# A hybrid attention block on one core: evicted halves share three slots, the scheduler's transfers share the wire by time, and attention is ordered anew

## Chip, core and metric

The kernel runs on one core of a Trainium2 chip, in one launch. The metric is the time of a launch on the device in microseconds (us), the median of several runs. Every time below comes from those runs or from one profiled execution.

## The reference, cut to what matters

Sequence 1024, width 1024, everything in float32.

```python
h = modulate(x, ...)                       # adaLN on RMSNorm
x = x + 0.5 * g1 * swiglu(h, w1, w3, w2)   # FFN 1, inner width 2816
h = modulate(x, ...)
z = h @ w_in                               # q, k, v of both branches, index parts, two gates
ya = fox_attention(fq, fk, fv, log_f)      # 8 heads of 64, causal, with forget bias
yb = dsa_attention(dq, dk, dv, iq, ik, iw, 256)  # 8 heads, one key head, top 256 of index scores
merged = sigmoid(ga) * (ya @ w_br_fox) + sigmoid(gb) * (yb @ w_br_dsa)
x = x + g2 * (merged @ w_out)
h = modulate(x, ...)
x = x + 0.5 * g3 * swiglu(h, w1, w3, w2)   # FFN 2
```

## The kernel before

Engines are named as in the profile: PE multiplies matrices, ACT applies functions and splits, DVE and POOL do elementwise work, SP and POOL issue the DMAs. Each float32 operand is split into a high and a low part (`wh`, `wl`, `h`, and in attention `pth`, `ptl`), and each product is three matmuls.

The program is recorded and then ordered. Every call on an engine becomes a task of a `Plan`; `flush` takes the tasks of a phase, and `place`, a list scheduler, simulates them with the costs of `length` and writes out an order per engine. Only the order goes into the program: on the chip every engine runs its instructions in that order and waits at semaphores. Times in the model decide nothing else. `FOUND` holds, for the flushes 1 to 5, one setting of the scheduler each, and seeds that move its keys. All instructions carry one line in the profile, L238.

There are six flushes: 1 is FFN 1, 2 the first projections of the mixer, 3 the index scores, 4 the top-k search with further projections and the first 16 gate blocks, 5 attention with 16 more gate blocks, 6 the branches, the output projection and FFN 2.

In flush 5, each of 32 steps (a pair of heads and a quarter of the queries) scores keys (`p`), exponentiates to `pr`, stores and reloads it as `pc`, transposes it (`pt<-ident_r,pc`), splits the transposed tile (ACT writes `pth`, DVE `ptl`), and sums values into one PSUM bank (`py<-pth,vst`, `py<-ptl,vst`). At the end of a step ACT evicts half of the bank into `yt`, DVE adds the other half to it, and POOL issues its store to `d_y`. A gate block fills a bank of the same pair (`py<-h,wh`, `py<-h,wl`), ACT takes its tanh into `gt`, and POOL issues its store to `d_gate`. There are two `py` banks in all.

The tiles of an evicted step and an evicted gate are of half size, and their slots are these (`gates` L1277, `att_values` L1465, and the layout of the pool L2496):

```python
t = tmp.tile([128, H], F32, tag="gt", name="gt", bufs=2)   # gates, flushes 4 and 5
t = p.tile([64, 512], F32, tag="yt", name="yt", bufs=1)    # att_values, flush 5
```

A slot is free again when the store that reads it has landed. In flush 4 the gates use the same code with a pool of its own ("topk") and 8 PSUM banks `pj`.

Of the kernel before, what the change touches and what calls it, by code (L numbers as in the profile page):

```python
# [10 lines left out]
F32 = mybir.dt.float32  # L11
F32R = mybir.dt.float32r
# [14 lines left out]
H = 512  # L27
# [157 lines left out]
def real(v):  # L185
    return v.real() if isinstance(v, View) else v


ISSUE = 0.55
RESTART = 0.09  # L190
EXTRA = {"tensor": 0.06, "gpsimd": 0.1}
PLANS = [(20, 0.0, 0, 10, 400, 60, 2), (6, 0.05, 0, 10, 600, 60, 2), (20, 0.15, 0, 4, 300, 30, 2), (10, 0.05, 0, 10, 400, 20, 1),
# [8 lines left out]
}  # L201


def moved(tasks, key, seeds):

    order = sorted(range(len(tasks)), key=lambda i: tasks[i].rank)
    for seed in seeds:
        rng = Random(seed)
        n = rng.choice((4, 12, 40, 120, 400))
        at = rng.randrange(len(order))  # L210
        e = rng.choice(Plan.ENGINES + (None,))
        d = rng.choice((-1.0, 1.0)) * rng.choice((0.2, 0.6, 2.0, 6.0))
        for i in order[at:at + n]:
            if e in (None, tasks[i].engine):
                key[i] += d


class Plan:
# [29 lines left out]
    def take(self, engine, op, a, kw, calls=None, took=0.0):  # L248
# [49 lines left out]
        if t.dma:  # L298
            t.port = False
        elif engine == "gpsimd":  # L300
            t.port = bool(sb)
        elif engine == "vector":
            if op in ("tensor_scalar", "tensor_copy", "reciprocal"):
                t.port = len(sb) == 1 and "accum_out" not in kw and writes[0].tile.pool.space != PSUM
            else:
                t.port = len(sb) >= 2
        else:
            t.port = False
        if engine == "tensor" and not took:
            m = a[2] if op == "matmul" else a[1]  # L310
            t.exact = m.tile.dt in (F32R, BF16) or any(o[0] == "bitcast" and F32R in o[1] for o in m.ops)

    def want(self, *tiles):

# [18 lines left out]
    def length(self, t, e):  # L333

        n = t.n
        if t.dma:
            return 0.06 if e == "sync" else ISSUE, 0.0
        if e == "tensor":
            if t.took:
                return t.took, 0.23  # L340
            if t.exact:
                d = max(0.04, 0.0133 + n / 2400.0)
            elif t.op == "transpose":
                d = n / 1174.0
            else:
                d = max(0.224, 0.009 + n / 595.0)
            return d, 0.23
        more = "accum_out" in t.kw
        if e == "scalar":
            ap = sum(isinstance(t.kw.get(x), View) for x in ("bias", "scale"))  # L350
            return (0.055 if t.near else 0.1) + n / 1200.0 + (0.16 if more else 0.0) + (0.06 if ap else 0.0), 0.14
        if e == "gpsimd":
            if t.op in ("tensor_scalar", "memset"):
                return 0.24 + n / 1230.0, 0.105
            return 0.06 + n / 440.0, 0.105
        if t.op == "tensor_tensor_scan":
            d = 0.15 + n / 480.0
        elif t.op == "tensor_tensor_reduce":
            d = 0.08 + n / 960.0
        elif t.op == "scalar_tensor_tensor" or more:  # L360
            d = 0.13 + n / 960.0
        elif t.op == "tensor_scalar" and t.port:
            d = 0.065 + n / 1920.0
        else:
            d = 0.068 + n / 960.0
        return max(0.075, d), 0.16

    def deadlines(self, slack):

# [43 lines left out]
    def place(self, tie, strict, spare, window, lead, hold, seeds=()):  # L413
# [16 lines left out]
        for t in tasks:  # L430
            if not t.left:
                insort(waiting[t.engine], (key[t.i], t.i))
        placed, order = [False] * len(tasks), []
        todo = sorted(range(len(tasks)), key=lambda i: tasks[i].rank)
        at, base = 0, max(free.values())

# [16 lines left out]
        while len(order) < len(tasks):  # L453
# [29 lines left out]
                return None  # L483
            s, t, e = best
            i, d = t.i, t.len
            if e == "tensor" and s > free[e] + 1e-9:
                s += RESTART
            end = s + d + t.lat
# [1 line left out]
                port[e] = s + d  # L490
            free[e] = s + d
            if t.dma:
                wire = max(wire, s + 1.3) + t.bytes / 345e3
                end = wire + 0.7
                if e == "sync":
                    free[e] = max(free[e], wire - 5.0)
            placed[i] = True
            waiting[e].remove((key[i], i))
            mine = []
# [766 lines left out]
def gates(k, ws, hf, tmp, ptile, fine=1, blocks=16):  # L1266

    nc = k.nc
    for b in range(blocks):
        w = next(ws)  # L1270
        tick(k)
        ps = ptile()
        for i, c in enumerate(proj_t(k, ps, w, hf)):
            if i % fine == fine - 1:
                tick(k)
                yield 0.6 if b < 2 else 1.06
        t = tmp.tile([128, H], F32, tag="gt", name="gt", bufs=2)  # L1277
        nc.scalar.activation(t, ps, AF.Tanh, scale=0.5)
        later(k, 2, lambda b=b, t=t: nc.gpsimd.dma_start(k.d_gate[b, :, hf * H:hf * H + H], t))
        yield  # L1280
    while k.tails:
        tick(k)
# [129 lines left out]
def att_values(k, p, heads, j, ps_t, ps_y):  # L1412

    nc = k.nc
    py = ps_y()
# [46 lines left out]
                step([(a, kb), (b, kb), (c, kb), (d, kb)], [(v, kb, whole, slice(0, 512), kb == 0, kb == 2 * j)])  # L1462
            yield
    done()
    t = p.tile([64, 512], F32, tag="yt", name="yt", bufs=1)  # L1465
    nc.scalar.activation(t, py[64:128, :], AF.Copy)
    nc.vector.tensor_add(t, py[0:64, :], t)
    nc.gpsimd.dma_start(heads[0].y.rearrange("(h p) t -> p h t", h=2)[:, :, j * 256:j * 256 + 256],
# [718 lines left out]
def layer(tc, xT, c, pos, ada_w, ada_b, ng, inv, w13a, w2a, w_a, w_f, w_q, w_g, fb, fg, dg, wbr, wout, w13b, w2b, out):  # L2187
    with ExitStack() as es:
# [304 lines left out]
        with ExitStack() as ph:  # L2493
            ap = pool(ph, "att", True)
            full, half = [128, T], [128, H]
            ap.lay(("mn", [128, 8], F32, 8), ("pth", half, F32R, PT), ("ptl", half, F32R, PT), ("yt", half, F32, 1),  # L2496
                   ("gt", half, F32, 2), ("big", full, F32, BIGS))
            mp = pool(ph, "masks", True)
            pp = pool(ph, "ps3", True, space=PSUM)
            p2 = lambda: pp.tile([128, T], F32, tag="p2", name="p2", bufs=2)  # L2500
            pt = lambda dt: pp.tile([128, H], dt, tag="pt", name="pt", bufs=2)
            py = lambda: pp.tile([128, H], F32, tag="py", name="py", bufs=2)
            def dsa():
                t = nat(k, k.d_dkv)
                k.dvs = v_stack(k, ap, t[:, :, 64:128])
                yield from k_parts(k, ap, lambda b: t[:, b, 0:64], 64, None, pt)
                k.dks = k.ks
                yield from attention(k, ap, "dsa", 4, k.d_y[1], p2, pt, py)

            weave((chain(attention(k, ap, "fox", 4, k.d_y[0], p2, pt, py), dsa()), 300), (behind(nc, masks(k, mp), 600), 40), (behind(nc, gates(k, ws, 1, ap, py, 1, 16 - LATE), 100), 130 - 9 * LATE))  # L2510
            nc.flush(k.hh[1] + k.hl[1] if LATE else ())
# [147 lines left out]
```

## Time and profile before

| what | value |
|---|---|
| median of 3 runs | 2133.44 us (2133.26 to 2134.06) |
| the profiled execution: its time | 2131.21 us |
| its span in the trace | 2129.5 us |
| PE busy | 2097.6 us (99%) |
| DVE busy | 1600.3 us (75%) |
| ACT busy | 1125.7 us (53%) |
| POOL busy | 354.7 us (17%) |

The span runs from the first to the last recorded event. The profiled execution took 1.7 us more than its span, and is 2.2 us below the median. Busy PE includes time in which its clock was lowered; the granted clock of a stretch stands beside it in the rows below, as a share of full speed.

### The profile page before, as it was taken

The numbers are of one execution on the slowest core, as the hardware profiler recorded it, in microseconds if no ns is written. First come the engines' busy times: TensorE is split into PE (matmuls) and PEld (weight loads), VectorE is DVE, ScalarE is ACT, GpSimd is POOL, SyncE is SP. The second block draws the span as 40 slices with busy tenths as digits, with TensorE's granted clock in tenths as the row PEclk, the third lists the DMA queues.
The fourth block names the chain that finished last, engine by engine and source line by source line (L and its number), as shares of the span: only waits on it lengthen the run. The fifth ranks groups of instructions, "written<-read, shape, count | busy, mean of one in ns | idle before, by whom it ended". The sixth has DMA issues, their size and how long they took to land.

```text
span 2129.5 us, 31818 instructions
## 1 busy us (share of the span) xinstructions
PE 2097.6 (99%) x10548; PEld 1750.9 (82%) x10548; DVE 1600.3 (75%) x3118; ACT 1125.7 (53%) x2088; POOL 354.7 (17%) x595
## 2 busy tenths in 40 slices
PE   7999999999999999999999999999999999999999
PEld 5888888888888999997777777878888888888887
DVE  7988877869976398775899876688876765548754
ACT  5744444445565286875776775234643333334443
POOL 0013323311101100001544432001011111000000
PEclk9999999999999999999999999999999999999999
DMA  9358877899842326457866757396143524166611
GB/s 357 110 165 284 288 277 265 281 385 336 295 147 109 113 96 220 155 188 250 280 236 229 244 205 272 124 363 201 45 144 104 193 66 152 60 227 248 227 65 55
DMA packets 207958, 429.20 MB, mean 202 GB/s; under 512 B 33192, under 2 KB 51624, under 8 KB 207792
## 3 DMA queue, kind: packets, MB, share of 16 engines
q1 hardware_dynamic: 175392, 321.49, 44.8%
q0 software_dynamic: 32400, 105.67, 13.4%
q8 instruction: 83, 1.36, 0.3%
q14 instruction: 83, 0.68, 0.1%
HBM read 279.48 MB, written 109.83 MB: 183 GB/s over the span
## 4 chain that ended last, share of the span: by engine, by line
PE 90%; DMA 3%; issue 3%; DVE 2%; ACT 1%; POOL 1%; SPq 0%; POOLq 0%; DVEq 0%; ACTq 0%
PE b L238 41%; PE y L238 29%; PE pj L238 10%; PE py L238 5%; PE p L238 3%; PE pt L238 2%; DMA pc<-pr 1%; DMA d_y<-yt 1%; POOL pr L238 0%; ACT tks L238 0%; DMA nat<-d_dkv 0%; DMA wr<-in_wout 0%; DVE ptl L238 0%; ACT pth L238 0%; DMA mraw<-in_ada_w 0%
## 5 line engine op out<-in xcount | busy, mean ns | idle before, releaser
L238 PE MATMUL b<-h,wh 128*128 128x512 f32 x1552 | 482.4, 391 | 1.9 <-ACT h L238 1.9
L238 ACT ACTIVATE wh<-wr 128x512 fp32r<-128x512 f32 x312 | 194.7, 629 | 363.1 <-PE b L238 154.8
L238 PE MATMUL y<-h,wh 128*128 128x512 f32 x1168 | 361.3, 389 | 0.0
L238 PEld LDWEIGHTS b<-h,wh 128*128 128x128 f32 x1552 | 292.0, 189 | 64.3 <-ACT h L238 2.0
L238 DVE TENSOR_TENSOR wl<-wr,wh 128x512 fp32r<-128x512 f32 x312 | 212.5, 688 | 141.9 <-ACT wh L238 140.2
L238 PE MATMUL b<-h,wl 128*128 128x512 f32 x776 | 302.8, 390 | 0.0
L238 PEld LDWEIGHTS y<-h,wh 128*128 128x128 f32 x1168 | 219.0, 188 | 46.1 <-ACT y L238 0.4
L238 PE MATMUL y<-h,wl 128*128 128x512 f32 x584 | 227.2, 389 | 0.0
L238 PE MATMUL pj<-wh,h 128*128 128x384 f32 (+1 forms) x768 | 175.1, 319 | 0.0
L238 PEld LDWEIGHTS b<-h,wl 128*128 128x128 f32 x776 | 146.0, 188 | 30.7
L238 POOL DMA_DIRECT2D d_g<-z x154 | 83.6, 543 | 501.3 <-DVE z L238 474.2
L238 DVE TENSOR_TENSOR wl<-a,wh 128x512 fp32r<-128x512 f32 x132 | 90.9, 688 | 70.4 <-ACT wh L238 64.2
L238 ACT ACTIVATE wh<-a 128x512 fp32r<-128x512 f32 x132 | 82.5, 625 | 103.3 <-PE b L238 58.7
L238 PE MATMUL b<-wh 128*128 128x512 f32 x352 | 136.5, 389 | 0.0
L238 PE MATMUL b<-wh,wl 128*128 128x512 f32 x352 | 136.5, 389 | 0.0
L238 PE MATMUL b<-wl,wh 128*128 128x512 f32 x352 | 136.5, 389 | 0.0
L238 ACT ACTIVATE wh<-g 128x512 fp32r<-128x512 f32 x154 | 95.9, 624 | 73.5 <-PE b L238 46.8
L238 PEld LDWEIGHTS pj<-wh,h 128*128 128x128 f32 x768 | 130.0, 189 | 0.8
L238 PEld LDWEIGHTS y<-h,wl 128*128 128x128 f32 x584 | 109.6, 188 | 22.9
L238 DVE TENSOR_TENSOR wl<-g,wh 128x512 fp32r<-128x512 f32 x154 | 105.7, 687 | 27.0 <-ACT wh L238 27.0
L238 PE MATMUL pj<-wl,h 128*128 128x384 f32 (+1 forms) x384 | 114.1, 318 | 0.0
L238 POOL TENSOR_SCALAR pr<-pr,mn 128x512 f32<-128x512 f32 (+7 forms) x128 | 96.9, 770 | 101.1 <-DVE mn L238 63.1
(389 smaller groups left out, 4423.2 us busy)
## 6 DMA issues: line engine op xcount, KB each, us to landing
d_g<-z POOLq DMA_DIRECT2D x154, 256.0 KB, 3.9
g<-d_g SPq DMA_DIRECT2D x154, 256.0 KB, 5.4
mraw<-in_ada_w SPq DMA_DIRECT2D x144, 256.0 KB, 5.3
wr<-in_w13a SPq DMA_DIRECT2D x112, 256.0 KB, 5.2
wr<-in_w13b SPq DMA_DIRECT2D x88, 256.0 KB, 5.0
pc<-pr SPq DMA_DIRECT2D x32, 448.0 KB, 4.6
a<-in_w2a SPq DMA_DIRECT2D x44, 256.0 KB, 6.1
a<-in_w2b SPq DMA_DIRECT2D x44, 256.0 KB, 5.9
```

The source lines that it names most:

```text
L238: getattr(getattr(self.tc.nc, engine), op)(*map(real, a), **{n: real(v) for n, v in kw.items()})
```

## The change

It has three parts. First, the model: transfers used to follow one another on one wire; the new function `carry` gives each the free time of the wire from its own start on, and start-up time and rate differ by flush (`WIRES`). An exact transpose costs .085 behind another transpose and .063 otherwise (`TURN`). A few costs of issue, ACT and DVE operations move. Second, `gt` and `yt` get one tag, `ev`, with three slots: in attention the same three half tiles as before, in flush 4 three where there were two. Third, `FOUND[5]`, the setting and seeds of the order of attention, is another.

```diff
-ISSUE = 0.55
+ISSUE = 0.68
+TURN = 0.063, 0.085
+WIRES = {1: (1.3, 375e3), 5: (2.0, 310e3)}
...
-    5: [(30, 0.0, 0, 0, 300, 1000000000.0, 2, (797680840, 247863689,
+    5: [(20, 0.02, 0, 2, 300, 1000000000.0, 2, (15049007, 346050216,
...
+def carry(busy, at, need):
+
+    i = len(busy)
+    while i and busy[i - 1][1] > at:
+        i -= 1
+    first, begin = i, at
+    while i < len(busy):
+        p, q = busy[i]
+        if p > at:
+            if p - at >= need:
+                break
+            need -= p - at
+        else:
+            begin = min(begin, p)
+        at = q
+        i += 1
+    at += need
+    busy[first:i] = [(begin, at)]
+    return at
...
-            if t.exact:
-                d = max(0.04, 0.0133 + n / 2400.0)
+            if t.turn:
+                d = TURN[0]
+            elif t.exact:
+                d = max(0.04, 0.0133 + n / 2400.0) + (0.004 if t.dear and n == 512 else 0.0)
...
-            return (0.055 if t.near else 0.1) + n / 1200.0 + (0.16 if more else 0.0) + (0.06 if ap else 0.0), 0.14
+            return (0.055 if t.near else 0.1) + n / 1200.0 + (0.12 if more else 0.0) + (0.06 if ap else 0.0) + (0.13 if t.calls[0][1][0].tile.kw.get("name") == "yt" else 0.0), 0.14
...
+            if e == "tensor":
+                if t.turn and turned:
+                    d = TURN[1]
+                turned = t.turn
...
-                wire = max(wire, s + 1.3) + t.bytes / 345e3
-                end = wire + 0.7
+                w = carry(busy, s + late, t.bytes / rate)
+                wire = max(wire, w)
+                end = w + 0.7
...
-        t = tmp.tile([128, H], F32, tag="gt", name="gt", bufs=2)
+        t = tmp.tile([128, H], F32, tag="ev", name="gt", bufs=3)
...
-    t = p.tile([64, 512], F32, tag="yt", name="yt", bufs=1)
+    t = p.tile([64, 512], F32, tag="ev", name="yt", bufs=3)
...
-            ap.lay(("mn", [128, 8], F32, 8), ("pth", half, F32R, PT), ("ptl", half, F32R, PT), ("yt", half, F32, 1),
-                   ("gt", half, F32, 2), ("big", full, F32, BIGS))
+            ap.lay(("mn", [128, 8], F32, 8), ("pth", half, F32R, PT), ("ptl", half, F32R, PT), ("ev", half, F32, 3),
+                   ("big", full, F32, BIGS))
```

Every engine has the same instructions before and after; their order and the slots differ. Nearly all of the difference lies in flush 5, with a smaller piece in flush 3; flush 6 and SP's order are nearly the same. The whole code is recorded at L261 after the change.

Two places matter below. The first is PE's order from flush 4 into attention: `pj` is the last gate block of flush 4, `nat` the stacked keys and values that are transposed first, `py<-h` the first gate block of flush 5. Before:

```order
L238 MATMUL pj<-h,wl 128x512
L238 MATMUL pt<-ident_r,nat 128x128 x2
L238 MATMUL py<-h,wh 128x512 x2
L238 MATMUL py<-h,wl 128x512
L238 MATMUL pt<-ident_r,nat 128x128 x6
L238 MATMUL py<-h,wh 128x512 x2
L238 MATMUL py<-h,wl 128x512
L238 MATMUL py<-h,wh 128x512 x2
```

With the change:

```order
L261 MATMUL pj<-h,wl 128x512
L261 MATMUL pt<-ident_r,nat 128x128 x8
L261 MATMUL py<-h,wh 128x512 x2
L261 MATMUL py<-h,wl 128x512
L261 MATMUL py<-h,wh 128x512 x2
L261 MATMUL py<-h,wl 128x512
L261 MATMUL py<-h,wh 128x512
L261 MATMUL p_10680<-kst,qs 128x128 x6
```

All eight transposes now stand ahead of the gate, and the first scores (`p`) follow after fewer matmuls of the gate.

The second place is ACT's order at the end of attention, where `yh<-yr` and `wh<-wr` are the first splits of flush 6. Before:

```order
L238 ACTIVATE gt<-py 128x512
L238 ACTIVATE pth<-pt 128x512 x2
L238 ACTIVATE yt<-py 64x512
L238 ACTIVATE pth<-pt 128x512
L238 ACTIVATE pth<-pt 128x256
L238 ACTIVATE gt<-py 128x512
L238 ACTIVATE yt<-py 64x512
L238 ACTIVATE yh<-yr 128x512
L238 ACTIVATE wh<-wr 128x512 x2
```

With the change:

```order
L261 ACTIVATE yt<-py 64x512
L261 ACTIVATE pth<-pt 128x512
L261 ACTIVATE pth<-pt 128x256
L261 ACTIVATE pth<-pt 128x512 x2
L261 ACTIVATE yt<-py 64x512
L261 ACTIVATE pth<-pt 128x256
L261 ACTIVATE yt<-py 64x512
L261 ACTIVATE gt<-py 128x512
L261 ACTIVATE yh<-yr 128x512
L261 ACTIVATE wh<-wr 128x512 x2
```

The last gate now stands behind the last `yt` instead of ahead of it, and the three last `yt` come closer together.

In flush 1, at start-up, ACT splits six weight tiles (`wh<-wr`) before the first `h` where it split four. On all of PE in flush 5, 486 of the 672 exact transposes stood directly behind another one, and 464 do with the change.

## Rows read from the trace of the kernel before

**Rows 1.** The page, first part: an engine's busy us, share of the span, instructions.

```profile
PE 2097.6 (99%) x10548; PEld 1750.9 (82%) x10548; DVE 1600.3 (75%) x3118; ACT 1125.7 (53%) x2088; POOL 354.7 (17%) x595
```

**Rows 2.** Busy time by stretch: start-up, flushes 1 to 4, attention (flush 5), flush 6. The columns are the stretch, its length, the busy us (and instructions) of PE, PE's weight loads, DVE, ACT and POOL, then the granted clock of PE, the share of the DMA engines, GB/s.

```profile
0.00:27.40 27.40, 16.70 (x52) 6.55 (x52) 15.52 (x39) 9.90 (x17) 1.16 (x7) 0.97 0.92 329
27.40:996.00 968.60, 968.54 (x4731) 837.60 (x4732) 769.45 (x1625) 556.25 (x1004) 159.61 (x298) 1.00 0.65 223
996.00:1312.00 316.00, 299.62 (x2180) 236.52 (x2179) 256.30 (x554) 228.74 (x501) 140.03 (x190) 0.99 0.72 247
1312.00:2125.00 813.00, 812.70 (x3588) 670.26 (x3587) 558.32 (x901) 330.78 (x569) 53.93 (x101) 1.00 0.45 154
```

**Rows 3.** What PE waited for between 996 and 1312 us: the waiting operation, what released it, us in total, times, longest us.

```profile
PE b L238 <- ACT wh L238: 3.8, 1, 3.8
PE py L238 <- DVE yt L238: 3.8, 4, 2.6
PE py L238 <- ACT gt L238: 2.4, 1, 2.4
PE pt L238 <- DMA pc<-pr: 1.7, 2, 1.1
PE pt L238 <- DVE ptl L238: 1.4, 4, 0.6
...
```

**Rows 4.** The timeline at the start of attention, of PE and then ACT: start, length, engine, line, operation, out and in, count, and the idle time before it with its releaser.

```profile
996.31 0.28 PE L238 MATMUL pt<-ident_r,nat 128*128 128x128 f32 x2
998.98 0.73 PE L238 MATMUL py<-h,wh 128*128 128x512 f32 x2 [2.39 <-ACT gt L238]
...
998.33 0.60 ACT L238 ACTIVATE gt<-pj 128x512 f32<-128x512 f32 x1 [5.89 <-DMA d_gate<-gt]
```

**Rows 5.** PE's timeline at the first late reload of a score tile.

```profile
1014.77 0.42 PE L238 MATMUL pt<-ident_r,pc 128*128 128x128 f32 x3 [1.11 <-DMA pc<-pr]
```

**Rows 6.** The timeline of POOL, ACT and PE around 1119 us.

```profile
1111.95 0.66 POOL L238 DMA_DIRECT2D d_y<-yt  x1
...
1118.40 0.59 ACT L238 ACTIVATE yt<-py 64x512 f32<-64x512 f32 x1 [3.47 <-DMA d_y<-yt]
...
1119.86 0.36 PE L238 MATMUL py<-pth,vst 128*128 128x256 f32 x1 [2.62 <-DVE yt L238]
```

**Rows 7.** Busy time by stretch, as in rows 2, behind three idle times of PE; the third number from the end is the granted clock.

```profile
1000.00:1005.00 5.00, 5.00 (x42) 4.12 (x41) 2.26 (x8) 1.68 (x3) 0.00 (x0) 1.00 1.00 366
...
1120.00:1125.00 5.00, 5.00 (x29) 3.90 (x29) 4.01 (x11) 2.93 (x11) 0.65 (x1) 0.66 0.62 249
...
1311.00:1316.00 5.00, 4.28 (x11) 3.26 (x12) 5.00 (x9) 5.00 (x11) 0.61 (x1) 0.66 0.61 152
1316.00:1320.00 4.00, 4.00 (x19) 3.29 (x18) 4.00 (x8) 4.00 (x8) 0.00 (x0) 1.00 0.96 346
```

**Rows 8.** How long ACT waited for earlier stores of `yt` between 960 and 1315 us (us, times, longest), and the view of the tile `yt`: us from the issue of its store to landing.

```profile
ACT yt L238 <- DMA d_y<-yt: 10.6, 7, 3.5
...
DMA to landing us min/median/max: 2.3/4.0/6.4
```

**Rows 9.** The same last line for the tile `gt` and its store.

```profile
DMA to landing us min/median/max: 2.3/5.2/8.9
```

**Rows 10.** The timeline of PE, ACT, POOL and DVE at the end of attention.

```profile
1304.86 0.47 PE L238 MATMUL py<-pth,vst 128*128 128x512 f32 x1 [0.74 <-DVE yt L238]
...
1307.48 0.39 PE L238 MATMUL py<-h,wl 128*128 128x512 f32 x1
1311.72 0.50 PE L238 MATMUL b<-yh,wh 128*128 128x512 f32 x1 [3.85 <-ACT wh L238]
...
1307.91 0.60 ACT L238 ACTIVATE gt<-py 128x512 f32<-128x512 f32 x1 [3.02 <-PE py L238]
1310.03 0.59 ACT L238 ACTIVATE yt<-py 64x512 f32<-64x512 f32 x1 [1.53 <-DMA d_y<-yt]
1310.53 0.62 ACT L238 ACTIVATE yh<-yr 128x512 fp32r<-128x512 f32 x1
...
1305.01 0.61 POOL L238 DMA_DIRECT2D d_y<-yt  x1 [6.04 <-DVE yt L238]
...
1313.07 4.29 DVE L238 TENSOR_TENSOR yl<-yr,yh 128x512 fp32r<-128x512 f32 x7
```

**Rows 11.** PE's timeline at two groups of transposes, each with the row that follows.

```profile
1115.62 0.85 PE L238 MATMUL pt<-ident_r,pc 128*128 128x128 f32 x8
1116.31 0.47 PE L238 MATMUL py<-h,wh 128*128 128x512 f32 x1
...
1288.05 0.22 PE L238 MATMUL pt<-ident_r,pc 128*128 128x128 f32 x1
1288.11 0.45 PE L238 MATMUL py<-h,wh 128*128 128x512 f32 x1
```

**Rows 12.** The timeline of the start-up, PE and ACT.

```profile
20.23 0.68 PE L238 MATMUL b<-ident,nr 128*128 128x128 f32 x4 [1.35 <-DVE nr L238]
...
23.25 2.17 ACT L238 ACTIVATE wh<-wr 128x512 fp32r<-128x512 f32 x4
```

**Rows 13.** Busy time by stretch, as in rows 2, within attention, and the sum over 1000 to 1300 us.

```profile
1050.00:1200.00 150.00, 143.81 (x1097) 116.48 (x1095) 137.97 (x289) 108.75 (x239) 71.82 (x95) 0.99 0.69 237
...
sum 300.00, PE 290.60 PEld 230.00 DVE 252.46 ACT 224.10 POOL 137.94; mean PE 96.87 PEld 76.67 DVE 84.15 ACT 74.70 POOL 45.98
```

More of the change, by code (lines that the diff above doesn't have):

```diff
@@ L308, in take @@
             t.port = False
+        t.turn = t.dear = False
         if engine == "tensor" and not took:
@@ L311, in take @@
             t.exact = m.tile.dt in (F32R, BF16) or any(o[0] == "bitcast" and F32R in o[1] for o in m.ops)
+            t.turn = t.exact and op == "transpose"
+            t.dear = a[0].tile.kw.get("tag") == "py"
     def want(self, *tiles):
@@ L365, in length @@
             d = 0.068 + n / 960.0
-        return max(0.075, d), 0.16
+        return max(0.09 if t.op == "reciprocal" else 0.075, d), 0.16
     def deadlines(self, slack):
@@ L432, in place @@
                 insort(waiting[t.engine], (key[t.i], t.i))
-        placed, order = [False] * len(tasks), []
+        placed, order, turned = [False] * len(tasks), [], False
+        busy = [(-1.0, wire)]
+        late, rate = WIRES.get(self.flushes, (1.3, 345e3))
         todo = sorted(range(len(tasks)), key=lambda i: tasks[i].rank)
@@ L492, in place @@
             if t.dma:
-                wire = max(wire, s + 1.3) + t.bytes / 345e3
-                end = wire + 0.7
+                w = carry(busy, s + late, t.bytes / rate)
+                wire = max(wire, w)
+                end = w + 0.7
                 if e == "sync":
-                    free[e] = max(free[e], wire - 5.0)
+                    free[e] = max(free[e], w - 5.0)
             placed[i] = True
```

2 rows, old and new, of the table FOUND are left out of this document.

## The prediction

> **What bounds the kernel now.** I read the page first [rows 1]: PE is busy 2097.6 of 2129.5 us, so no more than some 32 us can come from its idle time, and no other engine is near. Where that idle time lies is in the table by stretch [rows 2]. From 27.4 to 996 us PE is busy 968.54 of 968.60, and from 1312 to 2125 us 812.70 of 813. In these 1782 us an order can gain or lose only by adding a wait. The start-up leaves 10.7 us idle, attention 316 − 299.62 = 16.4 us. The change reorders attention, so it is these 16.4 us that are at stake, and what follows from them.
>
> The waits of PE in attention [rows 3] show four that are large: 3.8 for `wh` (once), 3.8 for `yt` (the longest 2.6), 2.4 for `gt` and 1.7 for reloads of `pc`; the rest are several under 0.7. The chains then tell who was late. At 998.98 PE waits for `gt`, and ACT had begun that `gt` only after 5.89 us behind the store of an earlier one [rows 4]. At 1119.86 PE waits for `yt`: its store was issued at 1111.95, and ACT could not write the single slot again until 1118.40, after 3.47 us of standing still [rows 6]. PE's wait is for DVE's name, but the releaser two steps back is a landing store. The same is behind the 0.74 at 1304.86, and half of the end: ACT does the last `yt` at 1310.03, 5.02 us after POOL issued the store before it at 1305.01, and `yh`, `wh` and PE at 1311.72 stand behind it [rows 10]. In all ACT waited 10.6 us for seven stores of `yt` [rows 8]. A reader should see one shape four times: a slot that comes back late, on an engine that is not the bound, reaches PE through an in-order queue.
>
> PE's clock makes two of these dearer. After the wait at 1119.86 the granted clock averages 0.66 over the next 5 us, and after the one before 1311.72 again [rows 7], where full speed is 2.4 GHz and the lower level 1.2. A mean of 0.66 over 5 us loses 5 × 0.34 = 1.7 us of work. After 998.98 the next 5 us are at 1.00, so nothing is lost there.
>
> **The change part by part.** *Three shared slots.* A store takes a median of 4.0 us from issue to landing, 6.4 at the most, for `yt` [rows 8], and 5.2 and 8.9 for `gt` [rows 9]. There are 48 evictions in the 316 us, one in 6.6 us on average; with a ring of three a slot is asked for some 3 × 6.6 = 20 us after it was filled, where the one `yt` slot could be asked for a few us later. I take all waits for slots as gone. That they go is not sure, since gates and steps now take each other's slots; the bound on the other side is that none goes.
>
> The Trainium skill speaks against this. The page "DMA: Bandwidth & Descriptors", section "Anatomy of one DMA — SWDGE (gpsimd) path", gives such a store about 2.0 us plus bytes over 436e3, an estimate of 2.3 us for 128 KB, by which one slot would have been back before ACT wanted it and the slot terms of the sum would be near nothing (the third rival below). The trace agrees only at the minimum, 2.3 us; its median is 4.0 and the store of 1111.95 held ACT to 1118.40 [rows 6, 8], so the rows decide.
>
> *Start of attention.* With three slots in flush 4 the last `gt` needs no landing, and eight transposes stand between `pj` and the gate's first matmul. The last `gt` takes 0.60 [rows 4] and is covered but for some 0.3 (0.60 less the first transposes, 0.28 for two). Gain 2.39 − 0.3, about 2.0; bounds 0 and 2.39.
>
> *The step at 1119.* 2.62 idle and 1.7 of clock: 4.3 [rows 6, 7]; bounds 0 and 4.3.
>
> *1304.86.* 0.74, taken as 0.7 [rows 10].
>
> *The late `pc` at 1014.77.* 1.11 [rows 5]. The first scores come earlier in the new order, since less of the gate stands ahead of them. A store and a reload on a full wire may still be late, so I take 0.6; bounds 0 and 1.1.
>
> *End of attention.* PE ends its last gate matmul at 1307.48 + 0.39 = 1307.87 and goes on at 1311.72: 3.85 [rows 10]. Without the landing, ACT goes `gt` at 1307.91, `yh` 0.50 later (the spacing of 1310.03 and 1310.53), and from `yh` to PE it is 1311.72 − 1310.53 = 1.19. That is 0.04 + 0.50 + 1.19 = 1.73, a gain of 2.1; bounds 0 and 3.85. The clock's 1.7 behind it [rows 7] is only partly to be had: DVE has seven `yl` in 4.29 us there, 0.61 each [rows 10], and PE waits on them anyway. I take 1.0; bounds 0 and 1.7.
>
> *Transposes.* Eight in a row take 0.69, 0.086 each; one between other matmuls takes 0.06 [rows 11]. 22 fewer stand behind another: 22 × 0.026 = 0.6, taken as 0.5.
>
> *What may be added.* One gate in the new order starts in a bank that was evicted just before it; that costs at most one eviction of a gate, 0.60 [rows 10]. I take 0.6 off. The small waits for `ptl`, `pth`, `kst` and `nat` (the rest of rows 3) are taken as unchanged.
>
> *The other flushes* are costed at nothing. PE's 968.54 of 968.60 and 812.70 of 813 us [rows 2] hide what ACT and DVE do there; without that cover a moved split would cost its own 0.54. At start-up, ACT does two more splits ahead of the first `h`, 2 × 0.54 = 1.1 if it were on the path, while a 1.35 wait of PE may go [rows 12]. I take 0, with −1.35 and +1.1 as bounds. POOL and SP issue the same stores and loads; that `d_y` stores come three together at the end matters only if a load of `yr` is late, and its users stand far behind.
>
> *Sum.* 2.0 + 4.3 + 0.7 + 0.6 + 2.1 + 1.0 + 0.5 = 11.2, less 0.6 is 10.6. Against the profiled execution, 2131.2 − 10.6 = 2120.6. That execution is 2.2 below the median of the runs, 2133.4, so the median to be expected is 2133.4 − 10.6, about 2123.
>
> **The rivals.** *First: the new order has waits of its own.* PE is idle 16.4 us in attention for reasons that are partly `ptl`, `pth` and `pc`; another order places these anew, and a wait of 2.6 us also cost 1.7 of clock. One new wait of that kind and some small ones give back half, 5.5 us: 2128. For it: every wait in the table is one that the old order did not foresee either. Against it: ACT, DVE and POOL have slack on average, and the new slots take away the longest waits of ACT.
>
> *Second, slower: DVE thins out PE.* From 1050 to 1200 us DVE is busy 137.97 of 150, 92%, while its mean over 300 us is 252.46, 84% [rows 13]. Should the new order of DVE reach only 84% in that stretch, its 138 us of work would take 164 instead of 150, 14 more; less 10.6 that is 3.4 slower, 2137. It decides from 10.6 us on, at 138/160.6 = 86%. Against it: PE is busy 143.81 in that stretch, so DVE follows PE rather than leads it.
>
> *Third: the change doesn't do what it says.* If stores are as short as their minimum of 2.3 us [rows 8], or if ACT would wait for PE where it now waits for the store, slots are not what PE waits for. Then only the transposes' 0.5 is left, about 2133. Against it: 6.4 us between a store's issue and its slot's next use, with PE's wait right behind [rows 6].
>
> **How the numbers follow.** The forecast has 0.58, its own range 2118 to 2127. The first rival has 0.21, the third 0.14, the second 0.07. Lower than 2118 would need all upper bounds at once (2.39, 3.85, 1.7, 1.35: about 5 more). For 8 in 10 the range must take in the forecast and the first rival's 2128 with its spread: 2117 to 2130.5. A measurement of this kernel can tell about 0.2%, 4.3 us, from no change, so faster means under 2129.1. The forecast and most of the first rival (0.19) lie there: 0.77. Same: the third rival and the rest, 0.16. Slower: the second, 0.07.
>
> **What would show it.** In the trace after, ACT should wait for no landing store in attention, PE's wait for `yt` should be below 0.5, its wait at the start of attention 0.3, and at the end some 1.7. PE's idle time in attention should fall from 16.4 to about 8 us, with one less stretch at a clock of 0.66. I am wrong if the waits for `yt` and `gt` go, but PE's idle time in attention does not fall: then the order, and not the slots, made them. I am also wrong if ACT waits for stores as before, or if flush 3 or 6 shows idle time of PE that was not there.

## The result and the profile after

The changed kernel takes 2113.80 us (median of 5 runs, 2111.75 to 2113.92) against 2133.44 (5 runs, 2131.31 to 2134.64); the ratio is 0.9905, with a 95% interval of 0.9891 to 0.9920. The forecast was 2123 with a range of 2117 to 2130.5: the direction was right, the gain was nearly twice as large, and the time lies outside the range. The profiled execution took 2113.91 us with a span of 2112.2, 17.3 less than the span of before. The medians lie 19.6 apart: the profiled execution of before was 2.2 below its median, that of the change is 0.1 above, so 2.3 us of the gain stand in neither trace.

The page and the busy times by stretch of the changed kernel, with the columns of [rows 1, 2]; the stretches end about at the first matmul of FFN 1, the last of flush 4, and the first of flush 6. The last line is attention before, cut at the same two matmuls.

```profile
PE 2090.3 (99%) x10548; PEld 1747.4 (83%) x10548; DVE 1593.7 (75%) x3118; ACT 1126.3 (53%) x2088; POOL 356.6 (17%) x595
...
0.00:26.70 26.70, 15.12 (x52) 6.16 (x52) 16.35 (x40) 11.47 (x19) 1.16 (x7) 0.99 0.92 327
26.70:997.40 970.70, 969.96 (x4731) 837.88 (x4732) 768.21 (x1624) 555.51 (x1002) 159.81 (x298) 1.00 0.65 223
997.40:1295.60 298.20, 293.44 (x2179) 234.21 (x2177) 252.22 (x553) 227.88 (x501) 141.55 (x190) 1.00 0.74 261
1295.60:2112.20 816.60, 811.79 (x3588) 669.13 (x3588) 556.90 (x903) 331.42 (x569) 54.12 (x101) 1.00 0.45 154
...
996.08:1311.72 315.64, 299.26 (x2179) 236.28 (x2177) 256.01 (x553) 228.46 (x501) 139.75 (x190) 0.99 0.72 248
```

I measure attention from the last matmul of flush 4 (before 996.08, after 997.42) to the first of flush 6 (1311.72 [rows 10], after 1295.60). It was 315.6 us and is 298.2: 17.5 less. What lies ahead of it is 1.3 longer, what follows is 1.2 shorter (there stood 1.7 of clock, [rows 7]). So the whole gain of the traces is in attention. PE's idle time there fell from 16.4 to 4.8, and its busy time by 5.8.

PE's waits in the same stretch, with the columns of [rows 3]:

```profile
PE b L261 <- ACT wh L261: 1.7, 1, 1.7
PE py L261 <- ACT yt L261: 0.8, 3, 0.3
PE pt L261 <- DVE ptl L261: 0.7, 2, 0.4
PE py L261 <- ACT gt L261: 0.6, 1, 0.6
PE pt L261 <- ACT gt L261: 0.4, 1, 0.4
PE py L261 <- ACT pth L261: 0.2, 1, 0.2
```

The four large ones of [rows 3] are gone but for 1.7 at the end and 0.4 of `gt` at the start. Among them is `pc`, which no slot explains, and no slot explains either that most of the small ones for `ptl` and `pth` went. The 0.6 for `gt` is new. Start and end of attention, PE and ACT, as in [rows 4, 10]:

```profile
997.85 0.60 ACT L261 ACTIVATE gt<-pj 128x512 f32<-128x512 f32 x1 [4.06 <-PE pj L261]
998.50 0.54 PE L261 MATMUL pt<-ident_r,nat 128*128 128x128 f32 x4 [0.40 <-ACT gt L261]
...
1293.91 0.60 ACT L261 ACTIVATE gt<-py 128x512 f32<-128x512 f32 x1 [0.33 <-PE py L261]
1294.41 0.62 ACT L261 ACTIVATE yh<-yr 128x512 fp32r<-128x512 f32 x1
1295.60 0.50 PE L261 MATMUL b<-yh,wh 128*128 128x512 f32 x1 [1.72 <-ACT wh L261]
```

Both are as the steps said: 0.40 where 0.3 was forecast, 1.72 where 1.73 was. ACT's `gt` now waits for PE, not for a store, and ACT waits for no store of `gt` or `yt` in all of attention, as the prediction had asked.

### The profile page after: what moved, and what is told of

Its sections match the earlier page's. It is cut to its first block, busy times and chain, and to the rows that moved or that the text cites. A ratio compares the mean times of both kernels' runs of the same rounds, so it can differ in the third digit from the quotient of the medians.

```text
span 2112.2 us, 31881 instructions
## 1 busy us (share of the span) xinstructions
PE 2090.3 (99%) x10548; PEld 1747.4 (83%) x10548; DVE 1593.7 (75%) x3118; ACT 1126.3 (53%) x2088; POOL 356.6 (17%) x595
## 4 chain that ended last, share of the span: by engine, by line
PE 92%; DMA 4%; DVE 3%; ACT 1%; issue 1%; SPq 0%; DVEq 0%; ACTq 0%
PE b L261 39%; PE y L261 27%; PE pj L261 13%; PE py L261 7%; PE p L261 4%; PE pt L261 3%; DMA a<-in_w2a 1%; DMA mraw<-in_ada_w 1%; DVE wl L261 0%; DVE h L261 0%; DMA nat<-d_qkv 0%; DMA wr<-in_w13a 0%; DMA wr<-in_wout 0%; DMA pre<-in_w_g 0%; DVE z L261 0%
## 5 line engine op out<-in xcount | busy, mean ns | idle before, releaser
L261 PE MATMUL b<-h,wh 128*128 128x512 f32 x1552 | 483.0, 391 | 2.7 <-ACT h L261 2.6
L261 ACT ACTIVATE wh<-wr 128x512 fp32r<-128x512 f32 x312 | 195.5, 630 | 368.6 <-PE b L261 157.4
L261 PE MATMUL y<-h,wh 128*128 128x512 f32 x1168 | 361.0, 389 | 0.0
L261 PEld LDWEIGHTS b<-h,wh 128*128 128x128 f32 x1552 | 292.1, 189 | 65.4 <-ACT h L261 2.7
L261 DVE TENSOR_TENSOR wl<-wr,wh 128x512 fp32r<-128x512 f32 x312 | 213.0, 687 | 148.6 <-ACT wh L261 148.3
L261 PE MATMUL b<-h,wl 128*128 128x512 f32 x776 | 303.1, 391 | 0.0
L261 PEld LDWEIGHTS y<-h,wh 128*128 128x128 f32 x1168 | 219.1, 188 | 46.1 <-ACT y L261 0.3
L261 PE MATMUL y<-h,wl 128*128 128x512 f32 x584 | 227.2, 389 | 0.0
L261 PE MATMUL pj<-wh,h 128*128 128x384 f32 (+1 forms) x768 | 175.5, 319 | 0.0
L261 PEld LDWEIGHTS b<-h,wl 128*128 128x128 f32 x776 | 146.2, 188 | 30.7
L261 POOL DMA_DIRECT2D d_g<-z x154 | 83.6, 544 | 502.0 <-DVE z L261 485.9
L261 DVE TENSOR_TENSOR wl<-a,wh 128x512 fp32r<-128x512 f32 x132 | 90.6, 687 | 63.6 <-ACT wh L261 61.6
L261 ACT ACTIVATE wh<-g 128x512 fp32r<-128x512 f32 x154 | 96.0, 624 | 78.2 <-PE b L261 49.1
L261 PE MATMUL b<-wl,wh 128*128 128x512 f32 x352 | 136.7, 389 | 0.6 <-DVE wl L261 0.6
L261 ACT ACTIVATE wh<-a 128x512 fp32r<-128x512 f32 x132 | 82.4, 624 | 102.2 <-PE b L261 55.5
L261 PE MATMUL b<-wh 128*128 128x512 f32 x352 | 136.8, 389 | 0.0
L261 PE MATMUL b<-wh,wl 128*128 128x512 f32 x352 | 136.5, 389 | 0.0
L261 PEld LDWEIGHTS pj<-wh,h 128*128 128x128 f32 x768 | 130.2, 189 | 0.8
L261 DVE TENSOR_TENSOR wl<-g,wh 128x512 fp32r<-128x512 f32 x154 | 105.5, 685 | 30.6 <-ACT wh L261 30.6
L261 PEld LDWEIGHTS y<-h,wl 128*128 128x128 f32 x584 | 109.6, 188 | 22.8
L261 PE MATMUL pj<-wl,h 128*128 128x384 f32 (+1 forms) x384 | 113.9, 318 | 0.0
L261 POOL TENSOR_SCALAR pr<-pr,mn 128x896 f32<-128x896 f32 (+7 forms) x128 | 95.2, 756 | 99.8 <-DVE mn L261 56.7
```

The costliest lines, as they stand in the source:

```text
L261: getattr(getattr(self.tc.nc, engine), op)(*map(real, a), **{n: real(v) for n, v in kw.items()})
```

## The experiments

Two theories were on record. **S**: the slots are the cause, as in the prediction. **M**: the gain comes from an order planned with truer costs, and slots are room for it.

### The slots alone, with the order frozen

In the first run the order of before is kept instruction for instruction on every engine, and only the places of the tiles change:

```diff
+    def share(self, places):
+        free, held = [(i, p) for i, p in enumerate(places)], {}
+        for n, (_, _, t, _, _) in enumerate(self.trace):
+            for x in t.new:
+                if x.kw.get("name") in ("gt", "yt"):
+                    free.sort()
+                    tag, x.slot = held[id(x)] = free.pop(0)[1]
+                    x.kw = dict(x.kw, tag=tag)
+            if t.dma:
+                for x in t.tiles:
+                    if id(x) in held:
+                        free.append((n + 9, held.pop(id(x))))
...
+        if self.flushes in (4, 5):
+            self.share((("gt", 0), ("gt", 1), ("gt", 2) if self.flushes == 4 else ("yt", 0)))
```

> The order of before, kept instruction for instruction on every engine; only the slots change: yt and gt draw from three shared half tiles, the one whose store was issued longest ago first (in flush 4 gt has three). Theory S (the slots were the cause, as in the prediction): the stalls behind d_y and d_gate go, 2.0 at the start, 4.3 at 1119, 0.7 at 1304, 1.5 to 2.1 at the end and about 1 of its clock, so 2122 to 2125 against 2133.4. Theory M (the gain comes from an order that was planned with truer costs; the slots are only room for it): the stalls move to the next late thing, 2127 to 2132.

Measured: 2122.74 us, ratio 0.9951 (0.9933 to 0.9968). That is 10.8 below the median of before on the same chip, 2133.5. PE's waits in attention, and the busy times of this stretch as in [rows 2]:

```profile
PE b L238 <- ACT wh L238: 2.3, 1, 2.3
PE py L238 <- DVE ptl L238: 2.0, 4, 0.9
PE pt L238 <- DMA pc<-pr: 1.9, 3, 1.2
PE pt L238 <- DMA nat<-d_qkv: 1.5, 1, 1.5
PE pt L238 <- DVE ptl L238: 1.4, 4, 0.6
PE p L238 <- DVE mn L238: 0.8, 1, 0.8
PE py L238 <- ACT gt L238: 0.6, 1, 0.6
PE py L238 <- DVE yt L238: 0.4, 2, 0.2
...
994.70:1304.30 309.60, 297.48 (x2178) 235.18 (x2176) 256.87 (x553) 228.86 (x501) 139.67 (x190) 1.00 0.73 252
```

The waits for slots go as S says: `gt` 2.4 to 0.6, `yt` 3.8 to 0.4, `wh` 3.8 to 2.3, and the mean granted clock is 1.00. The time is where S had put it, in part by luck, as the next lines show. 3.5 us of waits appear that were not there (`ptl` ahead of `py` 2.0 for 0.7, `nat` 1.7 in two waits for 0.5, `mn` 0.8, `pc` 0.2 more): attention takes 309.7 us, 6.0 less than before, and its idle time is 12.2. The rest of this run's gain is 1.6 behind attention and 1.4 ahead of it; the latter is the clock at the start of the program (last section) and not the slots. The gain at the start of attention did not last: the wait for `gt` is 1.8 shorter, and one for a load of `nat` that was not there takes 1.5 of it back 12 us later.

```profile
995.76 0.72 PE L238 MATMUL py<-h,wh 128*128 128x512 f32 x2 [0.56 <-ACT gt L238]
...
1007.48 0.85 PE L238 MATMUL pt<-ident_r,nat 128*128 128x128 f32 x8 [1.49 <-DMA nat<-d_qkv]
```

The second run asks whether sharing is needed. The old order again, but `yt` gets two of the three half tiles and `gt` one, and flush 4 keeps two `gt` slots:

```diff
+        free, held = {"gt": [(0, ("gt", 0))], "yt": [(0, ("yt", 0)), (1, ("gt", 1))]}, {}
```

> The order of before, kept instruction for instruction; in attention yt has two of the three half tiles and gt one, nothing is shared, and flush 4 keeps two gt slots. If sharing is not needed: the yt waits go as in old_order_shared (attention 310), and only the 2.4 us wait for gt at its start stays, so 2123 to 2126. If one gt slot is too few, ACT waits for d_gate in attention and the time is over 2128.

Measured: 2122.73 us, ratio 0.9952 (0.9937 to 0.9967). The one wait of ACT for a store of these tiles is the 5.9 us of `gt` at the start, as before; attention takes 310.4. PE waits 2.4 us for that `gt`, and the 1.5 for `nat` are not there. So on this order a second slot for `yt` does it, and neither sharing nor the third slot of flush 4 adds anything that shows.

The third run keeps the order of the change and gives `yt` two slots of its own and `gt` one in attention, in place of sharing three; flush 4 stays as in the change.

> The order of the change, kept instruction for instruction; only the slots change: of the same three half tiles gt has one of its own and yt two, where the change lets both draw from all three. (One yt slot, as before, isn't possible with this order: it has two yt alive at eight places.) Theory S: the waits for landing stores come back wherever a slot is asked for early, 3 to 8 us, 2117 to 2122. Theory M: the order leaves time between evictions, so 0 to 3 us, 2114 to 2117.

Measured: 2112.40 us, ratio 0.9901 (0.9880 to 0.9921), attention 298.2 as with the change. No more than chance lies between the two (2111.30 to 2114.31 here). This falls on M's side, even below its range: sharing is not what the new order lives on.

### Costs and slots apart, with orders searched anew

A new order has to be searched when costs or slots change, so for each pair I searched the seeds of attention with the same effort (about 5,000 orders, kept when the planned time fell), for four pairs twice. How long the orders of before and of the change had been searched is not known. The edits are the change's own lines, taken back. Without its wire, transfers follow one another as before:

```diff
-                w = carry(busy, s + late, t.bytes / rate)
-                wire = max(wire, w)
-                end = w + 0.7
+                wire = max(wire, s + 1.3) + t.bytes / 345e3
+                end = wire + 0.7
...
```

Without its operation costs, `ISSUE` is 0.55, `TURN` goes, and ACT's, DVE's and `py`'s terms are those of before. Old slots are `yt` 1 and `gt` 2. The setting ahead of the seeds is that of before where old costs meet old slots and where half of the costs is old, and that of the change in the other searches.

> The planner's costs of the change with the slots of before (one yt, two gt); seeds of attention searched anew for 700 s. The planner's own time for attention is 297.9 us, 17.2 more than the change's 280.7. Theory S: at least the four large stalls stay or are paid for elsewhere, 2128 to 2136. Theory M with slots as room: the planner sees the late slots and orders around them, the chip keeps its promise within some 17 us as with the change, so attention takes about 315 and the time is 2129 to 2133; if the costs alone make the gain, 2114 to 2122.

> Costs and slots of before, seeds of attention searched anew with the same effort (5,000 orders) as in the five runs that belong together. The planner's time for attention is 285.9 us. In the runs so far the chip took 30 to 36 us more than the old costs had planned (before 279.3 and 315.6, old costs with new slots 277.3 and 307.1). Theory M: so again, attention 316 to 322, 2133 to 2140. If the gap were a matter of before's own seeds, attention 303 to 308, 2120 to 2127.

> The planner's costs of before with the three shared slots; the seeds of attention searched anew, 700 s of search as in the two runs that belong with it. In the planner's own time attention then takes 277.3 us, 2.0 less than before's order. Theory S: the slots do it, 2117 to 2123, and ACT waits for no store. Theory M: the old costs promise what the chip doesn't keep (before's attention was planned at 279.3 and took 315.5), so attention takes 308 to 316 again, 2127 to 2134.

> The same as old_model_new_slots (costs of before, three shared slots), searched again from other random seeds; planned at 277.0 us. It shows how much the draw of the search moves a time. If the plan's gap belongs to the costs: attention 305 to 309, 2120 to 2125.

> Costs and slots of the change, seeds of attention searched anew with the same effort of 5,000 orders. The planner's time for attention is 283.7 us. With the new costs the chip took 17 to 19 us more than planned (the change 280.7 and 298.2, new costs with old slots 297.9 and 316.9). Theory M: attention 301 to 303, 2116 to 2119. If the change's time is luck of its seeds, attention is as with the old costs and new slots, 306 to 309, 2121 to 2125.

> The same as new_model_new_slots (costs and slots of the change), searched again from other random seeds; planned at 286.0 us. If the gap of 17.5 to 18 us belongs to the costs: attention 303 to 305, 2117 to 2121. If it is the draw: anything from 300 to 316.

> The change's slots and its costs of turns, issue, ACT and DVE, but transfers one behind the other on the wire, with the old start-up and rate, in all flushes; 5,000 orders searched, planned at 282.7 us. If the wire is what made the old costs promise too much: the chip takes 30 us more or over, attention 312 or more, 2126 to 2131. If the costs of the engines' operations were: 18 more, attention 300 to 302, 2115 to 2118.

> The same as old_wire_new_slots (the change's slots and operation costs, transfers one behind the other), searched again; planned at 283.5 us. If the gap of 25 us belongs to these costs: attention 307 to 310, 2120 to 2125.

> The reverse: the change's slots and its wire (transfers share it by time, start-up 2.0 and 310 GB/s in attention), but the old costs of transposes, issue, ACT and DVE; 5,000 orders searched, planned at 279.2 us. If the wire decides: 18 us more than planned, attention 296 to 299, 2112 to 2115. If the operations' costs decide: 28 to 30 more, attention 307 to 309, 2121 to 2125.

> The same as old_costs_new_slots (the change's slots and wire, the old operation costs), searched again; planned at 279.5 us. The first draw took 36.6 us more than planned, with 17 us at half the clock. If that belongs to these costs: attention 313 to 318, 2125 to 2132; if it was the draw: 300 to 310, 2114 to 2124.

Two more went on with longer searches, one from a part of the change's own seeds, the other from the second order with old costs and new slots:

> Slots and costs of the change for attention, another order searched for 6,000 orders from a part of the change's seeds, planned at 282.8 us; flush 1 planned with the old costs. If the planned time is true up to a constant (17.5, 17.7, 18.1 and 19.0 us in four runs): attention 300.2 to 301.0, flush 1 1.3 us shorter, 2113 to 2116. If the change's order was luck: attention 303 to 310.

> The change's slots with the costs of before, the order of old_model_new_slots_2 searched on for 13,000 more orders: planned at 274.6 us instead of 277.0, 2.4 less. If a longer search pays under the old costs too: attention falls from 302.7 to about 300, 2113. If the old costs don't rank orders (277.3 took 307.1, 277.0 took 302.7): attention anywhere from 302 to 310, 2115 to 2124.

In the table, "planned" is the planner's time for attention and "chip" is attention in the trace, in us. Three of these runs came out outside all that had been expected of them: the old wire's first draw (between its two cases), the old operations' first (slower than both) and the old costs' second (faster). Three missed a stated case by 1 us or less: attention in the new costs' longer search (299.3 for 300.2 to 301.0) and in the old wire's second draw (310.3 for 307 to 310), and the median of the new costs' second (2121.7 for 2117 to 2121). In the old costs' first draw ACT waited once for a store of `yt` (1.6 us), where S had no such wait.

| slots | costs | planned | chip | chip less planned | median | ratio (95%) |
|---|---|---|---|---|---|---|
| old | old (before) | 279.3 | 315.6 | 36.3 | 2133.4 | 1 |
| old | old, searched | 285.9 | 320.7 | 34.8 | 2135.0 | 1.0008 (0.9999 to 1.0018) |
| old | new | 297.9 | 316.9 | 19.0 | 2132.5 | 0.9992 (0.9981 to 1.0003) |
| new | old, first | 277.3 | 307.1 | 29.8 | 2122.8 | 0.9951 (0.9934 to 0.9968) |
| new | old, second | 277.0 | 302.7 | 25.7 | 2115.4 | 0.9911 (0.9896 to 0.9925) |
| new | old, second, longer | 274.6 | 304.6 | 30.1 | 2119.4 | 0.9934 (0.9919 to 0.9949) |
| new | old wire, first | 282.7 | 307.9 | 25.2 | 2120.7 | 0.9940 (0.9925 to 0.9955) |
| new | old wire, second | 283.5 | 310.3 | 26.8 | 2122.3 | 0.9942 (0.9927 to 0.9957) |
| new | old operations, first | 279.2 | 315.8 | 36.6 | 2127.4 | 0.9971 (0.9961 to 0.9981) |
| new | old operations, second | 279.5 | 305.1 | 25.6 | 2120.2 | 0.9935 (0.9920 to 0.9949) |
| new | new, first | 283.7 | 301.4 | 17.7 | 2116.1 | 0.9915 (0.9900 to 0.9930) |
| new | new, second | 286.0 | 304.1 | 18.1 | 2121.7 | 0.9944 (0.9927 to 0.9961) |
| new | new, longer | 282.8 | 299.3 | 16.5 | 2113.6 | 0.9906 (0.9889 to 0.9922) |
| new | new (the change) | 280.7 | 298.2 | 17.5 | 2113.8 | 0.9905 (0.9891 to 0.9920) |

Four things follow.

- *With the old slots nothing helps.* Three orders, under old and new costs, lie at 2132.5 to 2135.0; all eleven with the new slots lie below. Truer costs without slots gave 0.08%, inside the interval. They did order around the late slots: ACT waited 5.9 us for four stores of `yt`, where it had waited 10.6 for seven, but the 5.9 for `gt` stayed and attention was no shorter. So M in its strong form, that the costs alone make the gain, falls. M with slots as room had 2129 to 2133 for this run and S 2128 to 2136, so 2132.5 doesn't part these two; what parts them is the frozen order, which gained 10.8 without a new order.
- *The draw matters as much as the costs, at equal effort.* Old costs gave 2122.8 and 2115.4, new ones 2116.1 and 2121.7. After the first of each I would have said that the costs are worth 7 us; the second draws turn it round. Most of that turn lies behind attention, though: attention itself took 302.7 and 304.1 in the second draws, and what follows it 815.4 and 820.3; with the new costs PE waited 1.7 us for `wh` at the end, and the granted clock was 0.66 from 1300 to 1305 us.
- *What goes with the new costs is a plan that comes true.* Under the new costs the chip takes 16.5 to 19.0 us more than planned in all five orders, and a lower plan was a shorter attention each time. Under old or half-old costs the difference is 25 to 37, and 2.4 us less planned (the longer search) was 1.9 more on the chip. Part of this is the clock: half speed within attention cost nothing in four of the five orders with new costs (2.7 us in the one with old slots) and 1.7 to 7.0 in eight of the nine others; without it the differences are 16 to 18 and 22 to 35. The setting is not what parts them, since the three orders with old costs and the change's setting have 26 to 30. So as far as five orders tell, two of them akin, a long search pays under the new costs, and the change's order is the best planned one. The five orders with old costs, two of them with old slots, are ranked rightly too but for that one pair.
- *Neither half of the costs does it alone.* With only the wire or only the operations the difference stays at 25 or more. Why both are needed the runs don't say.

The busy times of attention in the two longer searches, new costs and then old, show the same in PE's idle time, 5.5 and 9.2 us:

```profile
996.50:1295.80 299.30, 293.81 (x2179) 234.78 (x2177) 253.33 (x553) 228.22 (x501) 139.63 (x190) 1.00 0.74 260
...
996.50:1301.10 304.60, 295.38 (x2178) 236.70 (x2176) 253.92 (x553) 229.44 (x501) 142.13 (x190) 0.99 0.73 255
```

### Flush 1 with the old costs

The change's attention begins 1.3 us later. In this run the old costs are used while flush 1 is planned, as in

```diff
+        n, old = t.n, self.flushes == 1
...
-            if t.turn:
+            if t.turn and not old:
```

> The change as it is, but flush 1 is planned with the old costs; attention's order is the change's, instruction for instruction. Between the change and before, the last projection of flush 4 came 1.3 us later with the change: 0.65 of it a wait for wl at 455 us and 0.4 between 130 and 190 us. If that is the costs' doing, those waits go and the time is 2111.5 to 2113; if it was chance of the run, it stays at 2113.8.

Measured: 2112.57 us, ratio 0.9905 (0.9890 to 0.9920). PE's waits from 26 to 900 us, in the change and then in this run:

```profile
PE b L261 <- ACT h L261: 2.6, 1, 2.6
PE b L261 <- DVE wl L261: 0.6, 1, 0.6
...
PE b L261 <- ACT h L261: 1.9, 1, 1.9
```

The waits go as expected, and attention keeps its order (298.7). Attention begins at 994.4 us instead of 997.4, of which 1.7 is the shorter stretch at half speed at the start of the program (last section). The median is 1.2 lower, which the intervals don't tell apart. No version here is measurably faster than the change.

## Why the prediction was wrong, step by step

**Right.** PE bounds the kernel, the stake is attention's idle time, and the stalls come from slots behind landing stores. Each wait behind a store went on the frozen order, where nothing else was changed, and with the change:

| term | forecast | old order, three slots | the change |
|---|---|---|---|
| start of attention, left to wait | 0.3 | 0.56 | 0.40 |
| the stall at 1119 and its clock | 4.3 | gone | gone |
| 1304.86 | 0.7 | gone | gone |
| end, left to wait | 1.73 | 2.35 | 1.72 |
| gained behind the end (clock) | 1.0 | 1.6 | 1.2 |
| late `pc`, the sum of waits | 1.1 left | 1.9 left | 0 |
| waits that are new | 0.6 | 3.5 | 0.6 (`gt` at 1089.67) |

The slot terms summed to 2.0 + 4.3 + 0.7 + 2.1 + 1.0 = 10.1; the frozen order gained 10.8 by its medians, and 9.0 by its trace, of which 1.4 is the start of the program. So the median close to the sum is luck: of what the waits set free, the new waits took 3.5 back.

The Trainium skill's page "DMA: Bandwidth & Descriptors", section "Anatomy of one DMA — SWDGE (gpsimd) path", gives such a store 2.3 us, an estimate by its fit; by this rule a second slot would have gained next to nothing. The change's own trace has 2.3, 4.3 and 7.0 us as minimum, median and maximum for `yt`, and the slots did gain; the rule agrees only with the shortest store.

**Wrong: the new order was costed at almost nothing.** Two steps carry it. "The small waits for `ptl`, `pth`, `kst` and `nat` (the rest of rows 3) are taken as unchanged", and of the reordering only `pc` (0.6) and the transposes (0.5) were counted. On the frozen order attention is 309.7 us, with the new order 298.2: the order is worth 11.5 on top of the slots (3.5 of it are the waits that the slots had laid bare in the old order), where the sum had 0.5 for it (1.1 with `pc`, less 0.6). Counted wait by wait against before, the small waits that were taken as unchanged fell from 4.5 us to 1.7, and the 1.65 of `pc` went whole, where 0.6 was forecast. I had priced the new order by what its rows show next to each other, and that tells only of what changes place by a row or two; whether a thousand rows meet their operands on time it doesn't tell.

**Mis-sized: what one wait costs.** The trace counts an idle time from the modelled end of the matmul before it. That matmul is shown at 0.39 us, though the next one follows 0.23 after it when nothing is waited for (the line below, from before; the next matmul starts at 996.31 [rows 4]).

```profile
996.08 0.39 PE L238 MATMUL pj<-h,wl 128*128 128x512 f32 x1
```

So each wait costs some 0.16 more than its idle time, and that part stands under busy. Counting idle times over 0.03 us in attention, there were 29 before and 13 after: 16 × 0.16 is an estimate of 2.6 of the 5.8 us by which busy time fell. The clock is another 1.7; 1.5 is left, where 0.5 was forecast for the transposes. They make up some 1.4 of it: from start to start, waits and half speed aside, one took 78.8 ns on average before and 76.7 with the change, and there are 672.

In sum, the 17.5 us of attention are 11.6 of idle time, 2.6 hidden behind it, 1.7 of clock and 1.5 of transposes and the like. The forecast had for these 7.4 (2.0 + 2.6 + 0.7 + 0.6 + 2.1 − 0.6), 0, 1.7 and 0.5. The 4.2 that are missing in the first are the small waits (2.8), `pc` (1.0) and gaps too short for the view of waits (0.3); the terms of the slots themselves, 7.4 in idle time, measured 7.5.

**The other steps.** Flushes 1 to 4 and the start, costed at 0, took 1.3. The forecast carried the gain from the profiled execution to the median as it was; the medians gained 2.3 more than the traces, and no trace shows why. Of the rivals, the first (new waits of the order's own) did happen to the old order with new slots, 3.5 us of them, and not to the new order; the second did not: from 1050 to 1200 us, where it had DVE fall to 84%, DVE is busy 140.36 of 150 us with the change (94%) and PE 148.32; the third is excluded by the frozen order. The range was set by the bounds of the waits that I had named; its lower end left out the waits that I had not, and the 2.3 of the medians; with the traces' 17.3 alone the median would have been 2116.1, still outside.

**Open.** Why the chip still takes 17 us more than the new costs plan, and why either half of the costs leaves 25, was not measured. Nor was the time that the new costs would plan for the order of before.

## What to carry to other kernels

When a change gives room and a new order together, price them apart: freeze the order and give the room, and then compare orders; here each was worth about half by the medians; by the traces, without the clock at the start of the program, some 7.6 us were the room's and 11 the order's. A planner's better costs are seen in how constant the chip's time less the planned time is over several orders, not in one time, since two draws of the same search differed by 1.6 to 7.3 us. Before slots are shared, try a second one for the tile whose stores land late: here that alone gave the frozen order its gain.

## What the hardware showed that was not expected

Two executions of the same work can differ by 1.7 us through the clock at the start of the program. Busy times from 23 to 34 us in before and in the first run with the frozen order; the granted clock is the third number from the end:

```profile
23.00:34.00 11.00, 9.02 (x39) 7.31 (x38) 9.67 (x18) 6.24 (x11) 0.00 (x0) 0.69 1.04 381
...
23.00:34.00 11.00, 9.00 (x38) 7.11 (x38) 9.75 (x18) 6.03 (x11) 0.00 (x0) 0.84 1.03 382
```

Both have the same instructions in the same order there. A mean of 0.69 over 11 us is 6.8 us at half speed (1.2 GHz), in the second it is 3.4, and the difference is worth 1.7 us of work at full speed; both lengths occur among the profiles of old and new orders alike. The change's five runs lie at 2111.75 and 2112.19, and at 2113.80 to 2113.92, which is the same distance; that these runs differ for this reason was not shown. Differences of this size are not told apart by three runs here.

The length of a wait alone does not tell whether the clock falls behind it. A wait of 2.17 us at 999.72 (old slots, new costs) and one of 1.72 at 1302.03 (old wire, first draw) were each followed by a mean granted clock of 0.66, from 1000 to 1005 and from 1302 to 1307 us; behind one of 2.41 at 999.24 (old order, two slots for `yt`) it stayed at 1.00.
